# A batched x·yᵀ on one Trainium2 core: products on four 64x64 tiles of TensorE, and stores of 4 MB as two 16 KB runs per partition

## The chip, the cores and the metric

The kernel runs on one core of one Trainium2 chip. The core has five engines with their own instruction streams: TensorE (PE, with its weight loads shown as PEld), VectorE (DVE), ScalarE (ACT), GpSimd (POOL) and SyncE (SP), and 16 DMA engines that carry data between HBM and the on-chip memory of 128 partitions. Engines wait for one another through semaphores. The metric is device time in microseconds; the time before is 301.73 us, the median of 3 runs (301.65 to 301.77).

## The reference

```python
def setup_inputs():
    batch, n_heads, seq_t, seq_s, channels = 8, 12, 512, 512, 64
    return {
        "x": np.random.randn(batch, n_heads, seq_t, channels).astype(np.float32),
        "y": np.random.randn(batch, n_heads, seq_s, channels).astype(np.float32),
    }

def reference(x, y):
    return np.einsum('bhtc,bhsc->bhts', x, y).astype(np.float32)
```

There are 96 heads. For each, a 512x64 matrix times the transpose of another 512x64 matrix gives 512x512 floats. The inputs are 2 x 12.6 MB, the output 100.7 MB.

## The kernel before

**Groups, halves, turns.** Sixteen heads form a group, and there are 6 groups (`NG`). A group of x or of y is 2 MB, laid out with 64 rows of 64 channels on each of the 128 partitions: a head takes 8 partitions. Half a group (8 heads, 64 partitions) is one turn of the products; there are 12 turns (`NH`). Each turn writes 8 MB of output as two stores of 4 MB, so there are 24 stores.

**Slots.** Three slots (`slots`) of 128 partitions x 32 KB serve two purposes. At the beginning each half of a slot is the landing place of one 2 MB load: the loads are numbered n = 0 to 11, x and y of group 0, x and y of group 1, and so on, six of them at once. Later a slot holds the 16 output rows per partition (`K = 16`) of one store. Everything moved by DMA is issued by SP on one queue: loads 0 to 5 at once, loads 6 to 11 each when its slot half has been cast (L146), then the 24 stores in order (L255), each when its slot has been filled.

**Casts (`compress`).** x of a group is cast from f32 to bf16 into `xk`, whole, by ACT (by POOL for the last group). y is cast by four instructions straight into an interleaved form (`yb`): DVE takes two, POOL one, and ACT or POOL the fourth. In `yb` two rows' values lie side by side in one 32-bit word.

**Mixing of x (`mix`).** Four copies a turn bring x into `xb`, one for each 32 of the turn's 64 partitions and each 32 channels. A value takes 16 bits of a 32-bit word; the other 16 are zero, from a memset of `xb` at the start, and which half of the word is filled depends on which group of four heads the value belongs to. POOL does these copies for the first two turns, DVE from then on.

**Transposes.** DVE's transposes work on 32x32 blocks of 32-bit words: the first half of `xb` into `xT0`, `yb` into `yT`, the second half of `xb` into `xT1`. Afterwards the contraction runs over 128 partitions: 64 channels for each of two groups of four heads. In a column of x that belongs to one group of heads, the 64 partitions of the other group hold the zeros.

**Products.** PE runs one hardware loop over the 12 turns (`products`). A unit is 8 matmuls, each with 128x64 weights from `xT` and 128x512 moving values from `yT`. Two run side by side, on the two 64-column halves of TensorE (`tile_position=(0, hs * 64)`). A unit fills four banks of PSUM (`pm0` or `pm1`, in turn). PE waits on `turned`, which DVE's transposes count up, and on `taken`, which ACT counts up as it empties `pm`.

**Evictions and stores (`unit`).** ACT copies each unit from PSUM into a quarter of a slot (128x2048 floats), and after four units SP issues the store. An eviction into a slot waits for the slot's previous store to land. The orders of all engines are written out by the loops at the end of the kernel; `emit` and `need` derive the waits from what is read and written. The store's view of the output is

```python
ov = out.rearrange("b h t s -> (b h t s)").rearrange(
    "(o u t q n) -> o t q u n", u=2, t=2, q=2 * Q * E, n=K * S
)
```

so that one store takes 128 runs of 32 KB, and neighbouring partitions (`u` = 0 and 1) write 4 MB apart.

Of the kernel before, what the change touches and what calls it, by code (L numbers as in the profile page):

```python
# [10 lines left out]
def kernel(  # L11
# [22 lines left out]
    nc = tc.nc  # L34
    B, H, T, C = x.shape
    _, _, S, _ = y.shape
    P = 128
    G = 16
    Q = P // G
# [1 line left out]
    NG = B * H // G  # L41
    NH = 2 * NG
    V = G // 4
    K = 16
    E = R // K
    D = 32
    U = K // 4
    SLOTS = 3
    fp32 = mybir.dt.float32
    bf16 = mybir.dt.bfloat16  # L50
# [4 lines left out]
    xv = x.rearrange("b h t c -> (b h t c)").rearrange("(g p n) -> g p n", p=P, n=R * C)  # L55
    yv = y.rearrange("b h t c -> (b h t c)").rearrange("(g p n) -> g p n", p=P, n=R * C)
    ov = out.rearrange("b h t s -> (b h t s)").rearrange(
        "(o u t q n) -> o t q u n", u=2, t=2, q=2 * Q * E, n=K * S
    )

    sb = ctx.enter_context(tc.tile_pool(name="sb", bufs=1))
    ps = ctx.enter_context(tc.tile_pool(name="ps", bufs=1, space=bass.MemoryType.PSUM))
    slots = [sb.tile([P, K * S], fp32, name=f"slot{i}") for i in range(SLOTS)]
    xks = [sb.tile([P, R, C], bf16, name=f"xk{i}") for i in range(NG - 1)]
    ybs = [[sb.tile([P, R // 2 * D], u32, name=f"yb{h}{i}") for i in range(NG - 1 + h)] for h in range(2)]
    xb = sb.tile([P, R * D], u32, name="xb")
    xTs = [sb.tile([P, K // 2 * D * E], u32, name=f"xT{i}") for i in range(2)]
    yT = sb.tile([P, D * R // 2], u32, name="yT")
    pms = [ps.tile([P, 4, S], fp32, name=f"pm{i}") for i in range(2)]
    engines = {"act": nc.scalar, "dve": nc.vector, "pool": nc.gpsimd, "pe": nc.tensor, "sp": nc.sync}  # L70
    sems, ticks, known, snaps, writer, readers = {}, {}, {e: {} for e in engines}, {}, {}, {}
    own = {e: {} for e in engines}
# [1 line left out]
    def sem(p):  # L74
        if p not in sems:
            sems[p] = tc.alloc_semaphore(p)
        return sems[p]
# [40 lines left out]

    asked = []

    def caster(n, half, ch):
        if n % 2 == 0:
            return "pool" if n == 10 else "act"
        return ("dve", "pool", "dve", "pool" if n > 8 else "act")[2 * half + ch]

    def copy(name, dst, src, reads, writes, tells=None, virtual=False):
        emit(
            name,
# [7 lines left out]
        )  # L136

    def space(n):
        i, j = divmod(n % (2 * SLOTS), 2)
        return slots[i][:, j * (K * S // 2):(j + 1) * (K * S // 2)], [("slot", i, 2 * j), ("slot", i, 2 * j + 1)]  # L140

    def load(n):
        to, where = space(n)
        emit(
            "sp",
            lambda: nc.sync.dma_start(to, (yv if n % 2 else xv)[n // 2]),  # L146
            writes=where,
            dma=f"in{n % (2 * SLOTS)}",
        )

    def compress(n):

        g = n // 2
        held, where = space(n)
        if n % 2 == 0:
            xk = g % (NG - 1)
            dst = xks[xk].rearrange("p r c -> p (r c)")
            copy(caster(n, 0, 0), dst, held, where, [("xk", xk)])
            return
        ys = held.rearrange("p (r c) -> p r c", c=C)  # L160
        for half in range(2):
            b = g % (NG - 1 + half)
            yv2 = ybs[half][b].bitcast(bf16).rearrange("p (j c w) -> p j w c", j=R // 2, w=2)
            for ch in range(2):
                copy(
                    caster(n, half, ch),
                    yv2[ch * 64:(ch + 1) * 64],
                    ys[half * 64:(half + 1) * 64, :, ch * D:(ch + 1) * D].rearrange(
                        "p (j w) c -> p j w c", w=2
                    ),  # L170
                    where,
                    [("yb", half, b, ch)],
                )

    def mix(i, name, part):

        g, half = divmod(i, 2)
        ch, u = divmod(part, 2)
        lo = half * 64 + u * D
        xk = g % (NG - 1)  # L180
        copy(
            name,
            xb[part * D:(part + 1) * D].bitcast(bf16).rearrange("p (r c u) -> p r c u", c=D, u=2)[:, :, :, u],
            xks[xk][lo:lo + D, :, ch * D:(ch + 1) * D],
            [("xk", xk)],
            [("xb", part)],
        )

    def transposes(i):
        g, half = divmod(i, 2)  # L190
        b = g % (NG - 1 + half)
        xe = xb.rearrange("p (e k c) -> p e k c", e=E, c=D)

        def of_x(kh):
            emit(
                "dve",
                lambda: nc.vector.transpose(  # L197
                    xTs[kh].rearrange("p (k r e) -> p e k r", r=D, e=E),
                    xe[:, :, kh * (K // 2):(kh + 1) * (K // 2), :],
                ),  # L200
                [("xb", part) for part in range(4)],
                [("xT", kh)],
                tells="turned",
            )

        of_x(0)
        emit(
            "dve",
            lambda: nc.vector.transpose(  # L209
                yT.rearrange("p (r j) -> p j r", r=D),  # L210
                ybs[half][b].rearrange("p (j c) -> p j c", c=D),
            ),
            [("yb", half, b, ch) for ch in range(2)],
            ["yT"],
            tells="turned",
        )
        of_x(1)

    def products():

        pe = mybir.EngineType.PE
        xcs = [t.bitcast(bf16).rearrange("p (k h m) -> p k h m", k=K // 2, h=V) for t in xTs]
        yc = yT.bitcast(bf16)
        nc.tensor.sem_inc(sem("taken"), 2)
        with nc.Fori(0, NH, engines=OrderedEngineSet([pe])) as turn:
            for t in range(2):
                for v in range(U):
                    done = t * U + v
                    if done in (0, U // 2):
                        nc.tensor.wait_ge(sem("turned"), turn * 3 + (2 + (done > 0)))  # L230
                    nc.tensor.wait_ge(sem("taken"), turn * (2 * U) + (done + 1))
                    for j in range(4):
                        kh, k = divmod(4 * v + j, K // 2)
                        for hs in range(2):
                            h = 2 * t + hs
                            last = nc.tensor.matmul(  # L236
                                pms[v % 2][hs * 64:(hs + 1) * 64, j, :], xcs[kh][:, k, h, :], yc[:, h * S:(h + 1) * S],
                                start=True, stop=True, tile_position=(0, hs * 64),
                            )
                    last.then_inc(sem("pe"), 1)  # L240

    def unit(o, v):

        i = o // 2
        pm = v % 2
        emit("pe", None, [("xT", v // 2), "yT"], [("pm", pm)], virtual=True)
        want = {"turned": 3 * i + (2 if o % 2 == 0 and v < 2 else 3), "taken": o * U + v + 1}
        assert all(want.get(p, 0) >= w for p, w in asked[-1].items()), (o, v, asked[-1])
        s = o % SLOTS
        rows = slots[s].rearrange("p (r s) -> p r s", s=S)[:, 4 * v:4 * v + 4, :]  # L250
        copy("act", rows, pms[pm], [("pm", pm)], [("slot", s, v)], "taken")
        if v == U - 1:
            emit(
                "sp",
                lambda: nc.sync.dma_start(ov[i, o % 2], slots[s]),  # L255
                reads=[("slot", s, w) for w in range(U)],
                dma=f"out{s}",
            )

    with tc.tile_critical():  # L260
        sem("taken")
        ticks["taken"] = 2
        for n in range(2 * SLOTS):
            load(n)
        emit("pool", lambda: nc.gpsimd.memset(xb, 0.0), writes=[("xb", part) for part in range(4)])  # L265
        for n in range(2 * NG):
            compress(n)
            if n < 2 * SLOTS:
                load(n + 2 * SLOTS)
            if n < 8:  # L270
                mix(n // 4, "pool", n % 4)
            if n == 3:
                transposes(0)
            if 6 < n < 11:
                for v in (0, 1) if n % 2 else (2, 3):
                    unit((n - 7) // 2, v)
            if n == 10:
                transposes(1)
        for part in range(4):
            mix(2, "dve", part)  # L280
        for i in range(1, NH):
            for o in (2 * i, 2 * i + 1):
                for v in range(U):
                    unit(o, v)
            if i + 1 < NH:
                transposes(i + 1)
            if i + 2 < NH:
                for part in range(4):
                    mix(i + 2, "dve", part)
        products()  # L290
        for name, o in (("pe", 2 * NH - 3), ("sp", 2 * NH - 2), ("act", 2 * NH - 1)):
            need(name, [(f"out{o % SLOTS}", ticks[f"out{o % SLOTS}"])])
# [30 lines left out]
```

## Time and profile before

| what | value |
|---|---|
| median of 3 runs | 301.73 us |
| the profiled execution, its own time | 301.98 us |
| its span | 300.2 us |
| mean granted TensorE clock | 0.748 |
| PE busy | 141.6 us (47%), 768 matmuls |
| DVE busy | 156.3 us (52%), 88 instructions |
| ACT busy | 203.6 us (68%), 106 instructions |
| POOL busy | 55.8 us (19%), 22 instructions |

The costliest groups of instructions, with the number of instructions, their busy time, the mean ns of one, the idle time of the engine just before them and what ended most of it:

```profile
L129 ACT ACTIVATE slot<-pm 128x2048 f32<-128x2048 f32 x96 | 174.4, 1879 | 54.1 <-DMA out_dram<-slot 42.7
L236 PE MATMUL pm<-yT,xT 128*64 128x512 bf16 x768 | 141.6, 520 | 133.7 <-ACT slot L129 77.4
...
L197 DVE STREAM_TRANSPOSE xT<-xb 128x1024 uint32<-128x1024 uint32 x24 | 48.2, 2009 | 36.0 <-PE pm L236 33.6
...
L209 DVE STREAM_TRANSPOSE yT<-yb 128x1024 uint32<-128x1024 uint32 x12 | 23.3, 1939 | 42.4 <-PE pm L236 42.4
```

A busy share is an average over a filling part (about the first 60 us, when the loads come in and POOL is at work) and a steady part (only stores). Idle time of an engine costs nothing as long as another resource sets the pace. A DMA's time "to landing" runs from its issue to its last byte and includes the time in which it stands behind earlier transfers.

### The profile page before, as it was taken

To read this page: it belongs to the slowest core of one execution; us is meant where nothing else is said; L and a number is where in the kernel's file an instruction comes from. 1 tells how busy PE (TensorE), PEld (TensorE's weight loads), DVE (VectorE), ACT (ScalarE), POOL (GpSimd) and SP (SyncE) were. 2 spreads that over 40 slices of the span, in tenths; PEclk is the share of its full clock that TensorE was granted. 3 is DMA by queue.
4 is the path that set the end of the run, shared out by engine and by line. 5 is a ranking of instruction groups with operands and counts; after the bars stand their busy time and mean duration, and the time that the engine had idled before them with its cause. 6 is when DMAs were issued, how large, how long until landed. Compare 5 with 4: busy or idle time off the path is not lost.

```text
span 300.2 us, 2037 instructions
## 1 busy us (share of the span) xinstructions
PE 141.6 (47%) x768; PEld 47.1 (16%) x768; DVE 156.3 (52%) x88; ACT 203.6 (68%) x106; POOL 55.8 (19%) x22
## 2 busy tenths in 40 slices
PE   0000314644866664847746467457483775644000
PEld 0000101211222211212212122112121221211000
DVE  0157874889894953826539447275393562500000
ACT  1665579875979868766876678667866696669000
POOL 2399299997000000000000000000000000000000
PEclk9999985597679786675866975877758577597555
DMA  7999999999999999999999999999999999999991
GB/s 271 428 434 432 426 428 428 430 426 450 450 424 419 419 454 450 424 419 420 450 442 428 424 419 445 445 428 428 419 450 441 428 424 419 450 441 428 424 424 83
DMA packets 5186, 125.85 MB, mean 419 GB/s; under 512 B 576, under 2 KB 576, under 8 KB 576
## 3 DMA queue, kind: packets, MB, share of 16 engines
q1 hardware_dynamic: 5184, 125.83, 97.7%
q14 instruction: 2, 0.02, 0.0%
HBM read 25.17 MB, written 100.66 MB: 419 GB/s over the span
## 4 chain that ended last, share of the span: by engine, by line
DMA 46%; ACT 19%; POOL 18%; PE 5%; DVE 3%; issue 1%; ACTq 0%; POOLq 0%; SPq 0%
DMA out_dram<-slot 44%; ACT slot L129 18%; POOL xb L131 8%; POOL yb L131 8%; PE pm L236 5%; DMA slot<-in_x_dram 3%; DVE xT L197 1%; DVE yT L209 1%; ACT xk L129 1%; POOL xk L131 1%; ACTq L92 0%; POOLq L92 0%; SPq L318 0%; SPq L260 0%
## 5 line engine op out<-in xcount | busy, mean ns | idle before, releaser
L129 ACT ACTIVATE slot<-pm 128x2048 f32<-128x2048 f32 x96 | 174.4, 1879 | 54.1 <-DMA out_dram<-slot 42.7
L236 PE MATMUL pm<-yT,xT 128*64 128x512 bf16 x768 | 141.6, 520 | 133.7 <-ACT slot L129 77.4
L236 PEld LDWEIGHTS pm<-yT,xT 128*64 128x64 bf16 x768 | 47.1, 138 | 227.6 <-ACT slot L129 145.2
L197 DVE STREAM_TRANSPOSE xT<-xb 128x1024 uint32<-128x1024 uint32 x24 | 48.2, 2009 | 36.0 <-PE pm L236 33.6
L131 DVE COPY xb<-xk 32x2048 bf16<-32x2048 bf16 x40 | 55.5, 1387 | 1.3
L209 DVE STREAM_TRANSPOSE yT<-yb 128x1024 uint32<-128x1024 uint32 x12 | 23.3, 1939 | 42.4 <-PE pm L236 42.4
L131 DVE CAST yb<-slot 64x2048 bf16<-64x2048 f32 x12 | 31.7, 2645 | 23.8 <-DMA slot<-in_y_dram 23.6
L131 POOL COPY xb<-xk 32x2048 bf16<-32x2048 bf16 x8 | 25.3, 3162 | 15.7 <-ACT xk L129 9.7
L129 ACT ACTIVATE xk<-slot 128x4096 bf16<-128x4096 f32 x5 | 18.1, 3617 | 13.8 <-DMA slot<-in_x_dram 13.8
L131 POOL CAST yb<-slot 64x2048 bf16<-64x2048 f32 x8 | 24.9, 3118 | 0.9
L129 ACT ACTIVATE yb<-slot 64x2048 bf16<-64x2048 f32 x4 | 9.8, 2460 | 5.1 <-DMA slot<-in_y_dram 5.1
L131 POOL CAST xk<-slot 128x4096 bf16<-128x4096 f32 x1 | 3.6, 3595 | 0.1
L265 POOL MEMSET xb<- 128x2048 uint32 x1 | 1.8, 1805 | 0.5 <-SPq L260 0.5
L129 ACT ACT_TABLE_LOAD x1 | 1.3, 1283 | 0.9 <-SPq L260 0.9
L307 POOL MEMSET const-float32-0.0<- 128x1 f32 x1 | 0.1, 98 | 0.2 <-issue 0.2
L307 POOL MEMSET const-bfloat16-1.0<- 128x1 bf16 x1 | 0.1, 100 | 0.0
L307 POOL MEMSET const-uint8-127<- 128x1 uint8 x1 | 0.1, 100 | 0.0
L307 POOL MEMSET const-float32-1.0<- 128x1 f32 x1 | 0.1, 98 | 0.0
## 6 DMA issues: line engine op xcount, KB each, us to landing
out_dram<-slot SPq DMA_DIRECT2D x24, 4096.0 KB, 22.0
slot<-in_x_dram SPq DMA_DIRECT2D x6, 2048.0 KB, 25.4
slot<-in_y_dram SPq DMA_DIRECT2D x6, 2048.0 KB, 22.2
```

The lines of the kernel that those rows point to most:

```text
L129: lambda: nc.scalar.activation(dst, src, COPY)
L131: else engines[name].tensor_copy(dst, src),
L197: lambda: nc.vector.transpose(xTs[kh].rearrange("p (k r e) -> p e k r", r=D, e=E), xe[:, :, kh * (K // 2):(kh + 1) * (K // 2), :],),
L209: lambda: nc.vector.transpose(yT.rearrange("p (r j) -> p j r", r=D), ybs[half][b].rearrange("p (j c) -> p j c", c=D),),
L236: last = nc.tensor.matmul(pms[v % 2][hs * 64:(hs + 1) * 64, j, :], xcs[kh][:, k, h, :], yc[:, h * S:(h + 1) * S], start=True, stop=True, t ...
L265: emit("pool", lambda: nc.gpsimd.memset(xb, 0.0), writes=[("xb", part) for part in range(4)])
L307: nc = _bacc.Bacc("TRN2", target_bir_lowering=False, num_devices=1)
```

## The change

The zeros go. x and y are both cast whole into bf16 (`xks`, and new `yks`), ACT taking x of the first four groups and POOL all y and the last two x. `mix` now interleaves both: eight copies of 32x2048 a turn, all on DVE, two rows' values side by side in a word for x as for y. The two groups of four heads lie on the two 64-partition halves, so a product contracts over 64 partitions with 64x64 weights, and TensorE is used as four 64x64 tiles (`tile_position=(t * 64, hs * 64)`). `xb` and `xT` are half as large, and so are the two x transposes. Four neighbouring matmuls (`t` and `hs`) go to four tiles and two PSUM banks. The memset is gone.

A slot is now 2 x 8 rows (`K = 8`), one half for each group of heads, and a unit writes two rows into each half. A store is 4 MB as before, but each partition's 32 KB go out as two runs of 16 KB, 4 MB apart. The turn's units are ordered by pairs of heads `o`. The six late loads are issued in the same order, each after one cast of the slot half. In the filling part, the first evictions into a slot wait for the casts of both its halves. PE counts up a semaphore (`mark`) that nothing waits for, once per unit.

```diff
-    K = 16
+    K = 8
...
-    U = K // 4
+    U = K // 2
...
-        "(o u t q n) -> o t q u n", u=2, t=2, q=2 * Q * E, n=K * S
+        "(i t o p n) -> i o p t n", t=2, o=2, p=P, n=K * S
...
-    slots = [sb.tile([P, K * S], fp32, name=f"slot{i}") for i in range(SLOTS)]
+    slots = [sb.tile([P, 2, K, S], fp32, name=f"slot{i}") for i in range(SLOTS)]
     xks = [sb.tile([P, R, C], bf16, name=f"xk{i}") for i in range(NG - 1)]
-    ybs = [[sb.tile([P, R // 2 * D], u32, name=f"yb{h}{i}") for i in range(NG - 1 + h)] for h in range(2)]
-    xb = sb.tile([P, R * D], u32, name="xb")
-    xTs = [sb.tile([P, K // 2 * D * E], u32, name=f"xT{i}") for i in range(2)]
-    yT = sb.tile([P, D * R // 2], u32, name="yT")
-    pms = [ps.tile([P, 4, S], fp32, name=f"pm{i}") for i in range(2)]
+    yks = [sb.tile([P, R, C], bf16, name=f"yk{i}") for i in range(NG - 1)]
+    xb = sb.tile([P, R // 2 * D], u32, name="xb")
+    yb = sb.tile([P, R // 2 * D], u32, name="yb")
+    xTs = [sb.tile([P, K // 4 * D * E], u32, name=f"xT{i}") for i in range(2)]
+    yT = sb.tile([P, R // 2 * D], u32, name="yT")
+    pms = [ps.tile([P, 2, 2, S], fp32, name=f"pm{i}") for i in range(2)]
...
+        g, b = n // 2, n // 2 % (NG - 1)
+        name = "pool" if n % 2 or n > 7 else "act"
+        to = (yks if n % 2 else xks)[b].rearrange("p r c -> p (r c)")
+        at = ("half", n % (2 * SLOTS))
+        copy(name, to, held, [at], [("yk" if n % 2 else "xk", b)])
+        if n >= 2 * NG - 2 * SLOTS:
+            for w in where:
+                readers.setdefault(w, []).extend(readers[at][-1:])
+
+    def mix(i):
+
+        g, half = divmod(i, 2)
+        b = g % (NG - 1)
+        for kind, held, to in (("x", xks[b], xb), ("y", yks[b], yb)):
+            pairs = to.bitcast(bf16).rearrange("p (j c w) -> p j w c", j=R // 2, w=2)
+            for part in range(4):
+                u, ch = divmod(part, 2)
+                lo = half * 64 + u * D
                 copy(
...
+                    "dve",
+                    pairs[part * D:(part + 1) * D],
+                    held[lo:lo + D, :, ch * D:(ch + 1) * D].rearrange("p (j w) c -> p j w c", w=2),
+                    [(kind + "k", b)],
+                    [(kind + "b", part)],
                 )
...
+                    nc.tensor.sem_inc(sem("mark"), 1)
+                    kh, k = divmod(v, U // 2)
+                    for w in range(2):
+                        for t in range(2):
+                            rows = slice(t * 64, (t + 1) * 64)
+                            for hs in range(2):
+                                h = 2 * o + hs
+                                last = nc.tensor.matmul(
+                                    pms[v % 2][hs * 64:(hs + 1) * 64, t, w, :],
+                                    xcs[kh][rows, k, w, h, :], yc[rows, h * S:(h + 1) * S],
+                                    start=True, stop=True, tile_position=(t * 64, hs * 64),
+                                )
...
-        copy("act", rows, pms[pm], [("pm", pm)], [("slot", s, v)], "taken")
+        copy("act", slots[s][:, :, 2 * v:2 * v + 2, :], pms[pm], [("pm", pm)], [("slot", s, v)], "taken")
...
-                lambda: nc.sync.dma_start(ov[i, o % 2], slots[s]),
+                lambda: nc.sync.dma_start(ov[i, o % 2], slots[s].rearrange("p t k s -> p t (k s)")),
...
-        emit("pool", lambda: nc.gpsimd.memset(xb, 0.0), writes=[("xb", part) for part in range(4)])
...
-            if n < 8:
-                mix(n // 4, "pool", n % 4)
-            if n == 3:
+            if n == 1:
+                mix(0)
                 transposes(0)
-            if 6 < n < 11:
-                for v in (0, 1) if n % 2 else (2, 3):
+                mix(1)
+            if n > 6 and n % 2:
+                for v in range(U):
                     unit((n - 7) // 2, v)
-            if n == 10:
+            if n == 9:
                 transposes(1)
-        for part in range(4):
-            mix(2, "dve", part)
+                mix(2)
...
             if i + 2 < NH:
-                for part in range(4):
-                    mix(i + 2, "dve", part)
+                mix(i + 2)
```

More of the change, by code (lines that the diff above doesn't have):

```diff
@@ L119 @@
     asked = []
[L121 to L124, printed above, removed]
     def copy(name, dst, src, reads, writes, tells=None, virtual=False):
@@ L138, in space @@
     def space(n):
-        i, j = divmod(n % (2 * SLOTS), 2)
-        return slots[i][:, j * (K * S // 2):(j + 1) * (K * S // 2)], [("slot", i, 2 * j), ("slot", i, 2 * j + 1)]
+        i, t = divmod(n % (2 * SLOTS), 2)
+        return slots[i][:, t].rearrange("p k s -> p (k s)"), [("slot", i, v) for v in range(U)]
     def load(n):
-        to, where = space(n)
+        to, _ = space(n)
         emit(
@@ L146, in load @@
             lambda: nc.sync.dma_start(to, (yv if n % 2 else xv)[n // 2]),
-            writes=where,
+            writes=[("half", n % (2 * SLOTS))],
             dma=f"in{n % (2 * SLOTS)}",
@@ L151, in compress @@
     def compress(n):
-        g = n // 2
         held, where = space(n)
[L155 to L164, printed above, removed]
-                copy(
[L166 to L172, printed above, removed]
-                )
@@ L175, in mix @@
[L175 to L187, printed above, removed]
+        g, b = n // 2, n // 2 % (NG - 1)
+        name = "pool" if n % 2 or n > 7 else "act"
@@ L189, in transposes @@
     def transposes(i):
-        g, half = divmod(i, 2)
-        b = g % (NG - 1 + half)
         xe = xb.rearrange("p (e k c) -> p e k c", e=E, c=D)
+        kk = K // 4
         def of_x(kh):
@@ L198, in of_x @@
                     xTs[kh].rearrange("p (k r e) -> p e k r", r=D, e=E),
-                    xe[:, :, kh * (K // 2):(kh + 1) * (K // 2), :],
+                    xe[:, :, kh * kk:(kh + 1) * kk, :],
                 ),
@@ L210, in transposes @@
                 yT.rearrange("p (r j) -> p j r", r=D),
-                ybs[half][b].rearrange("p (j c) -> p j c", c=D),
+                yb.rearrange("p (j c) -> p j c", c=D),
             ),
-            [("yb", half, b, ch) for ch in range(2)],
+            [("yb", part) for part in range(4)],
             ["yT"],
@@ L221, in products @@
         pe = mybir.EngineType.PE
-        xcs = [t.bitcast(bf16).rearrange("p (k h m) -> p k h m", k=K // 2, h=V) for t in xTs]
+        xcs = [t.bitcast(bf16).rearrange("p (k h m w) -> p k w h m", k=K // 4, h=V, w=2) for t in xTs]
         yc = yT.bitcast(bf16)
@@ L225, in products @@
         with nc.Fori(0, NH, engines=OrderedEngineSet([pe])) as turn:
-            for t in range(2):
+            for o in range(2):
                 for v in range(U):
-                    done = t * U + v
+                    done = o * U + v
                     if done in (0, U // 2):
@@ L231, in products @@
                     nc.tensor.wait_ge(sem("taken"), turn * (2 * U) + (done + 1))
[L232 to L239, printed above, removed]
+                    nc.tensor.sem_inc(sem("mark"), 1)
[10 more added lines that the diff above has]
+                                )
                     last.then_inc(sem("pe"), 1)
@@ L245, in unit @@
         pm = v % 2
-        emit("pe", None, [("xT", v // 2), "yT"], [("pm", pm)], virtual=True)
-        want = {"turned": 3 * i + (2 if o % 2 == 0 and v < 2 else 3), "taken": o * U + v + 1}
+        emit("pe", None, [("xT", v // (U // 2)), "yT"], [("pm", pm)], virtual=True)
+        want = {"turned": 3 * i + (2 if o % 2 == 0 and v < U // 2 else 3), "taken": o * U + v + 1}
         assert all(want.get(p, 0) >= w for p, w in asked[-1].items()), (o, v, asked[-1])
         s = o % SLOTS
-        rows = slots[s].rearrange("p (r s) -> p r s", s=S)[:, 4 * v:4 * v + 4, :]
-        copy("act", rows, pms[pm], [("pm", pm)], [("slot", s, v)], "taken")
+        copy("act", slots[s][:, :, 2 * v:2 * v + 2, :], pms[pm], [("pm", pm)], [("slot", s, v)], "taken")
         if v == U - 1:
@@ L264 @@
             load(n)
[L265 removed]
         for n in range(2 * NG):
             compress(n)
[L268 removed]
+            if n < 2 * NG - 2 * SLOTS:
                 load(n + 2 * SLOTS)
[L270 to L272 removed]
+            if n == 1:
+                mix(0)
                 transposes(0)
[L274 to L275 removed]
+                mix(1)
+            if n > 6 and n % 2:
+                for v in range(U):
                     unit((n - 7) // 2, v)
[L277 removed]
+            if n == 9:
                 transposes(1)
[L279 to L280 removed]
+                mix(2)
         for i in range(1, NH):
@@ L283 @@
                 for v in range(U):
-                    unit(o, v)
+                    if o > 2:
+                        unit(o, v)
             if i + 1 < NH:
```

## The prediction, made before the changed kernel ran

> **What bounds the kernel now.** I read the page's transfer rows first, because the span is 300.2 us and the whole traffic is fixed by the problem: 25.17 MB in, 100.66 MB out.
>
> ```profile
> DMA  7999999999999999999999999999999999999991
> ...
> q1 hardware_dynamic: 5184, 125.83, 97.7%
> ...
> HBM read 25.17 MB, written 100.66 MB: 419 GB/s over the span
> ```
>
> The 16 DMA engines are occupied in every slice but the first and the last, for 97.7% of the span. All 36 transfers go through one queue, so the time is: first packet, then 125.83 MB at the engines' pace, then the end of the slowest engine. The next view cuts the span into stretches (columns: PE, PEld, DVE, ACT, POOL busy, granted clock, DMA share, GB/s): all loads, then stores alone, then the end.
>
> ```profile
> 10.00:60.00 50.00, 11.88 (x54) 3.92 (x56) 32.70 (x14) 36.75 (x15) 40.84 (x13) 0.83 1.01 429
> 85.00:280.00 195.00, 115.40 (x638) 38.64 (x634) 100.94 (x64) 145.29 (x80) 0.00 (x0) 0.74 1.00 432
> 292.50:295.00 2.50, 0.00 (x0) 0.00 (x0) 0.00 (x0) 0.00 (x0) 0.00 (x0) 0.50 0.55 236
> 295.00:297.50 2.50, 0.00 (x0) 0.00 (x0) 0.00 (x0) 0.00 (x0) 0.00 (x0) 0.50 0.06 26
> ```
>
> Two things are to be seen. Loads, whose packets are 16 KB, run at 429 GB/s; stores, whose packets are 32 KB, at 432. And the end is ragged: in the last row the share is 0.06, which is one engine of sixteen, still writing when fifteen have finished. The packet records behind this view give the sizes: on fifteen engines successive 32 KB store packets start 1,209 to 1,210 ns apart all the way; on one engine they start 1,234 ns apart on average, but only while the cores compute (from 280 us on it is back to about 1,210). Over 192 store packets that is 192 x 24 ns = 4.6 us, part of which it had gained before: it ends at 298.6 us, the others at 294.0 to 294.7.
>
> Is the queue ever short of work? The chain of waits and the waits of the queue's own engine answer it:
>
> ```profile
> 218.25 21.95 DMA out_dram<-slot
> ...
> 240.29 1.89 ACT slot L129
> 242.17 0.04 issue
> 242.22 1.94 PE pm L236 x8
> 244.15 0.02 issue
> 244.18 3.65 ACT slot L129 x2
> ...
> 247.85 22.04 DMA out_dram<-slot
> ```
>
> ```profile
> SPq L255 <- ACT slot L129: 220.6, 24, 12.9
> ```
>
> The chain shows a slot's round: a store takes 22 us from issue to landing, then evictions refill the slot in about 7.6 us. SP waits 220.6 us for ACT, which looks like a bound and is none: a 4 MB store needs 4.19 MB / 432 GB/s = 9.7 us by itself, so at its issue 22.0 - 9.7 = 12.3 us of earlier stores stand before it. An eviction that comes 12 us late costs nothing.
>
> **The change, part by part.**
>
> *Stores as two 16 KB runs per partition.* Each 4 MB store becomes 256 packets instead of 128, so each engine writes 24 x 16 = 384 store packets in place of 192. No 16 KB write exists in the trace; the nearest row is the 16 KB load. Its starts are 607.7 ns apart where the loads run cleanest (10 to 20 us) and 611.5 ns between 30 and 60 us. Two of them against one 32 KB packet: 2 x 607.7 - 1,209.4 = 6.0 ns, or 2 x 611.5 - 1,210 = 13 ns. Per engine that is 192 x 6.0 = 1.15 us, or 192 x 13 = 2.5 us. The coarse rates agree: 100.66 MB at 429 instead of 432 GB/s is 234.6 against 233.0, 1.6 us. Lower bound: 0, if what the loads lose is the reading of HBM and not the packet. A gain I exclude, since no row shows a smaller packet moving more. I take 1.15 us, the cleanest stretch, where the fewest other things ran. All of it lies on the path, because the queue is never empty.
>
> The Trainium skill, page "DMA: Bandwidth & Descriptors", section "Latency and other measured facts", speaks against this part: it reports rows 4 MiB apart falling to 103 GB/s. Here the two runs of a partition are 4 MB apart. The row: the stores of now already send neighbouring partitions (`u`) 4 MB apart and run at 432 GB/s. By the rule the stores would take 100.66 MB / 103 GB/s = 977 us; I go by the row, since packets that alternate between the two regions are already what is measured.
>
> *The lagging engine.* What slows it the trace does not say; it goes with computing. After the change the same bytes are written while the same 768 matmuls and 96 evictions run, with DVE's count up from 88 instructions to 132 and POOL's down. I take the lag as it is, 4 us. Bounds: 0 (it vanishes, -4 us) and, if the loss is per packet and not per time, double (+4.6 us). For the range I take a third of each side as reachable.
>
> *DVE does all mixing.* Before, DVE interleaves x alone (4 copies a turn) and casts part of y. Now 8 copies of 32x2048 a turn, 96 in all, plus three transposes, of which the two x ones have half the elements. The price of a copy into this interleaved pattern is in two rows:
>
> ```profile
> L131 DVE COPY xb<-xk x40: 1296/1320/3420, 71.1 to 244.0; 32x2048 bf16<-32x2048 bf16 x40
> ...
> L131 DVE CAST yb<-slot x12: 1296/2912/3454, 13.6 to 67.6; 64x2048 bf16<-64x2048 f32 x12
> ```
>
> The cast has exactly the new nesting (32, 2, 32) on the output side; it runs at 1,296 ns when POOL is quiet (the one at 36.61 us) and up to 3,454 beside POOL. So 1.32 us with POOL idle, 3.45 at most beside it. In steady state, POOL has finished by about 70 us: 8 x 1.32 + 1.94 (y transpose) + 2 x 1.0 (half of 2,009 ns) = 14.5 us a turn. A turn's two stores need 19.4 us. Hidden under the stores; cover left 4.9 us a turn, and 12.3 us of queued stores behind that.
>
> *TensorE on four 64x64 tiles.* A unit is still 8 matmuls of 512 columns, now four at a time instead of two: 0.97 us or so instead of 1.94 at the low clock (the chain's x8 row). If the row halves don't overlap it stays at 1.94. Either way it sits beside ACT's 1.88 us per unit, and PE was idle half the span. Nothing on the path. After the last unit of a turn, 1.94 (y transpose) + 0.2 + 1 us pass before ACT has new work, against 1.88 of its own still running, so ACT's turn is about 8 x 1.83 + 1.3 = 16 us, under 19.4. The semaphore increment `mark` adds 8 PE instructions a turn there.
>
> *The fill.* POOL now casts every y (3.6 us by its x row; 5.0 if slowed like its y casts, 3.3 against 2.45), ACT the first four x. The evictions of store 0 now wait for both halves of their slot: y of group 3 lands at 43 (DVE's wait for it ends at 42.95), cast by 46.6 to 48, four evictions of 1.88 us, so store 0 is issued at 54 to 55.5; before it was at 57.0. The queue's loads end at 61.6 to 62. On DVE: first y cast by 17.2 to 18.6, then 8 copies beside POOL for about a third of the time (8 x 1.32 to 8 x 2.2 = 11 to 18 us) and 4 us of transposes; the first products start at 32 to 40, ahead of 47. Store 1 waits for y of group 4 (lands 52.7, cast by 58): 65.5 against 71.3 needed. Store 2: y of group 5 by 68, evictions by 75.5 against 81. SP passes loads 6 to 11 in the same order, each behind one cast: 12.3, 18.6, 22.1, 28.4, 31.9, 38.2 at the latest, none much later than now (last one 43.7). POOL loses the 1.8 us memset and the x copies. No packet comes later for any of it.
>
> **Sum.** Span 300.2 + 1.15 = 301.4; the profiled execution's own time was 301.98 against a median of 301.73, 0.25 above, so I add the change to the median: 301.73 + 1.15 = 302.9 us.
>
> **Rivals.**
> 1. *Not slower: the lagging engine catches up.* Place: the end, 294.7 to 298.6. Price up to -3.9 us. For it: the lag exists only beside computing, and PE's busy time falls from 141.6 us to perhaps half. Against: ACT's work and the number of instructions stay. From a cut of 1.15 us of the 3.9 (30%) it decides the sign; with two thirds gone, 301.73 + 1.15 - 2.6 = 300.3 us.
> 2. *The smaller packets cost nothing,* the loads' pace being HBM reading: 301.7 us. For it: the fit of 6 ns is small; against: the clean stretch shows it on all sixteen engines.
> 3. *DVE becomes the bound:* copies at 2.4 us instead of 1.32 even with POOL idle. Then a turn is 8 x 2.4 + 4 = 23.2 us; ten turns from 62 us, then 4 + 16 + 12 for the last: 330 us. Against: the 1,296 ns row with that nesting. The four products not overlapping at all (8 x 0.43 = 3.4 us a unit, 27.5 a turn) would end above that, near 380.
> 4. *The lag is per packet* and doubles: 302.9 + 4 = 307.
>
> **Chances.** Forecast 0.58; rival 1 0.17, rival 2 0.13, rival 4 0.06, rival 3 0.06. The time is the forecast's, 302.9. Its own range, from the packet's 0 to 2.5 us and a tenth of the lag, is 301.8 to 304.4; with a third of the lag on each side the range that holds 8 in 10 is 300.9 to 305.2. About 0.2% (0.6 us) is what a measurement here can tell from no change: slower than 302.3 has 0.70 (forecast, 3, 4), within 0.2% 0.13 (rival 2), faster 0.17.
>
> **What would show it.** Store packets of 16 KB with the stores' stretch at 429 to 431 GB/s: the packet step. Store packets starting 605 ns apart or less: wrong (rival 2). A last stretch with share 0.06 of about 4 us: the lag as it is; 0.06 absent or twice as long: rivals 1 or 4. DVE copies near 1.32 us and DVE idle waiting for PE: hidden; DVE never idle and a DMA digit below 9 in the middle: rival 3. A store 0 issued after 61.6 us would make the fill wrong.

## The result, and the profile after

The changed kernel takes 302.88 us (median of 6 runs, 302.63 to 303.42) against 301.75 us for the one before on the same chips (301.65 to 302.15): ratio 1.0037, 95% interval 1.0024 to 1.0050. It is slower by 1.1 us, about as forecast. The profiled execution took 302.99 us with a span of 301.2 us.

First the DMA's share and the transfer row of the page, then the stretches of the stores (columns: length, the five engines' busy time and counts, granted clock, DMA share, GB/s), after and, behind it, before. A packet is counted whole in the row in which it starts.

```profile
DMA  7999999999999999999999999999999999999993
...
q1 hardware_dynamic: 8256, 125.83, 98.3%
```

```profile
85.00:180.00 95.00, 40.27 (x316) 9.51 (x312) 68.61 (x54) 69.30 (x39) 0.00 (x0) 1.00 1.01 430
200.00:280.00 80.00, 32.04 (x248) 7.14 (x240) 42.68 (x33) 57.48 (x32) 0.00 (x0) 1.00 1.01 426
...
292.50:295.00 2.50, 0.00 (x0) 0.00 (x0) 0.00 (x0) 0.00 (x0) 0.00 (x0) 1.00 1.03 439
295.00:297.50 2.50, 0.00 (x0) 0.00 (x0) 0.00 (x0) 0.00 (x0) 0.00 (x0) 1.00 0.36 151
297.50:300.00 2.50, 0.00 (x0) 0.00 (x0) 0.00 (x0) 0.00 (x0) 0.00 (x0) 1.00 0.05 20
```

```profile
85.00:180.00 95.00, 57.68 (x330) 19.79 (x328) 56.24 (x36) 72.40 (x40) 0.00 (x0) 0.75 1.00 431
200.00:280.00 80.00, 45.67 (x246) 14.95 (x242) 33.67 (x22) 58.21 (x32) 0.00 (x0) 0.71 1.00 433
...
297.50:300.00 2.50, 0.00 (x0) 0.00 (x0) 0.00 (x0) 0.00 (x0) 0.00 (x0) 0.50 0.00 0
```

The queue carries 8,256 packets instead of 5,184, the 3,072 more that two runs per partition make. It is still never empty. The stores run at 430 GB/s up to 180 us and at 426 after 200 us; before, the same two stretches had 431 and 433. The end is as ragged as it was, nearly one engine's 0.06 in the last row, only later. The packet records give each packet's start, duration and size but not its engine; strung together by their times they make sixteen rows of packets. Fifteen engines end at 296.2 us (the median of them) instead of 294.2, and the late one at 299.6 instead of 298.6. So the path moved by 1.0 us, while the other fifteen engines lost 2.0.

DVE's work and its waits:

```profile
L127 DVE COPY xb<-xk x48: 1277/1296/4700, 12.2 to 243.1; 32x2048 bf16<-32x2048 bf16 x48
...
L127 DVE COPY yb<-yk x48: 1280/1301/4655, 20.9 to 248.5; 32x2048 bf16<-32x2048 bf16 x48
```

```profile
DVE yT L195 <- PE pm L225: 52.1, 11, 5.9
```

A copy takes 1.30 us in the steady part, and DVE waits 4.7 us a turn for PE (52.1 us over 11 turns): the copies are hidden. The slowest copies, beside POOL, took 4.7 us, longer than the 3.45 that I had as their bound; the reason is told below.

### The profile page after: what moved, and what is told of

The parts are those of the page before. It is cut to its first block, busy times and chain, and to the rows that moved or that the text cites. A ratio compares the mean times of both kernels' runs of the same rounds, so it can differ in the third digit from the quotient of the medians.

```text
span 301.2 us, 2167 instructions
## 1 busy us (share of the span) xinstructions
PE 99.9 (33%) x768; PEld 23.4 (8%) x768; DVE 189.8 (63%) x132; ACT 188.1 (62%) x101; POOL 31.3 (10%) x12
## 3 DMA queue, kind: packets, MB, share of 16 engines
q1 hardware_dynamic: 8256, 125.83, 98.3%
## 4 chain that ended last, share of the span: by engine, by line
DMA 69%; ACT 19%; POOL 2%; SPq 1%; issue 0%; ACTq 0%
DMA out_dram<-slot 51%; ACT slot L125 19%; DMA slot<-in_y_dram 18%; POOL yk L127 2%; SPq L142 1%; ACTq L93 0%; SPq L305 0%; SPq L249 0%
## 5 line engine op out<-in xcount | busy, mean ns | idle before, releaser
L125 ACT ACTIVATE slot<-pm 128x2048 f32<-128x2048 f32 x96 | 172.4, 1884 | 64.2 <-DMA out_dram<-slot 54.0
L225 PE MATMUL pm<-yT,xT 64*64 64x512 bf16 x768 | 99.9, 627 | 175.8 <-ACT slot L125 120.2
L127 DVE COPY xb<-xk 32x2048 bf16<-32x2048 bf16 x48 | 69.8, 1453 | 13.7 <-ACT xk L125 12.2
L127 DVE COPY yb<-yk 32x2048 bf16<-32x2048 bf16 x48 | 72.5, 1511 | 1.5
L195 DVE STREAM_TRANSPOSE yT<-yb 128x1024 uint32<-128x1024 uint32 x12 | 23.3, 1944 | 52.1 <-PE pm L225 52.1
L225 PEld LDWEIGHTS pm<-yT,xT 64*64 64x64 bf16 x768 | 23.4, 140 | 251.5 <-issue 251.5
L125 ACT ACTIVATE xk<-slot 128x4096 bf16<-128x4096 f32 x4 | 14.5, 3617 | 24.9 <-DMA slot<-in_x_dram 24.9
L183 DVE STREAM_TRANSPOSE xT<-xb 128x512 uint32<-128x512 uint32 x24 | 26.2, 1090 | 1.8 <-PE pm L225 1.5
L127 POOL CAST yk<-slot 128x4096 bf16<-128x4096 f32 x6 | 22.8, 3792 | 33.0 <-DMA slot<-in_y_dram 32.8
L127 POOL CAST xk<-slot 128x4096 bf16<-128x4096 f32 x2 | 8.3, 4175 | 1.5 <-DMA slot<-in_x_dram 1.5
```

The costliest lines, as they stand in the source:

```text
L125: lambda: nc.scalar.activation(dst, src, COPY)
L127: else engines[name].tensor_copy(dst, src),
L183: lambda: nc.vector.transpose(xTs[kh].rearrange("p (k r e) -> p e k r", r=D, e=E), xe[:, :, kh * kk:(kh + 1) * kk, :],),
L195: lambda: nc.vector.transpose(yT.rearrange("p (r j) -> p j r", r=D), yb.rearrange("p (j c) -> p j c", c=D),),
L225: last = nc.tensor.matmul(pms[v % 2][hs * 64:(hs + 1) * 64, t, w, :], xcs[kh][rows, k, w, h, :], yc[rows, h * S:(h + 1) * S], start=True, ...
```

## The experiments

Each run's time stands beside that of the kernel before on the same chip, 301.77 to 301.83 us. Where the end of the queue is given, it is from the packet records of the profiled execution: the median end of the fifteen engines, and the end of the late one. Where an experiment changes only into how many runs a partition's 32 KB are split, rows of the output land in other places than the reference has them.

**One run per partition again.** The changed kernel's computing with the old packets.

```diff
-        "(i t o p n) -> i o p t n", t=2, o=2, p=P, n=K * S
+        "(i o p n) -> i o p n", o=2, p=P, n=2 * K * S
...
-                lambda: nc.sync.dma_start(ov[i, o % 2], slots[s].rearrange("p t k s -> p t (k s)")),
+                lambda: nc.sync.dma_start(ov[i, o % 2], slots[s].rearrange("p t k s -> p (t k s)")),
```

> The changed kernel, but each partition's 32 KB of a store go to one contiguous run of the output (rows land in other places than the reference has them; bytes, stores and everything before them are the same). Theory (each extra store packet costs 5 to 6 ns of every DMA engine, the slowest one included, and nothing else of the change reaches the path): 1.1 us back, 301.6 to 302.0, store packets 1,210 ns apart, the last engine at about 298.6 us. Rival (the casts, copies and 64x64 products cost the time, or the lagging engine changed with them): stays at 302.7 to 303.2.

Measured: 302.19 us (301.99 to 302.68), ratio to before 1.0013 (1.0004 to 1.0023). Neither theory alone: 0.7 us of the 1.1 comes back, 0.4 us stays. The fifteen engines are back at 294.1 us, but the late one ends at 299.0, later than the 298.6 of before.

```profile
295.00:297.50 2.50, 0.00 (x0) 0.00 (x0) 0.00 (x0) 0.00 (x0) 0.00 (x0) 1.00 0.06 26
297.50:300.00 2.50, 0.00 (x0) 0.00 (x0) 0.00 (x0) 0.00 (x0) 0.00 (x0) 1.00 0.03 13
```

This is the end of that run: one engine alone in both rows, where in the kernel before no packet starts in the second. Fifteen engines end as before and the late one 0.4 us later, so the new computing lengthens the lag.

**Two runs in the kernel before.** The mirror image: old computing, new packets.

```diff
-        "(o u t q n) -> o t q u n", u=2, t=2, q=2 * Q * E, n=K * S
+        "(i t o p n) -> i o p t n", t=2, o=2, p=P, n=K * S // 2
...
-                lambda: nc.sync.dma_start(ov[i, o % 2], slots[s]),
+                lambda: nc.sync.dma_start(ov[i, o % 2], slots[s].rearrange("p (t n) -> p t n", t=2)),
```

> The kernel before, with its stores written as two 16 KB runs 4 MB apart (rows land in other places than the reference has them; all else as before). Theory: 302.6 to 303.2, all of the change's loss without any of its computing. Rival: 301.7, as before. In either case it shows whether the packets' wider spacing after about 180 us (607 to 614 ns), which the changed kernel's records have, belongs to the 16 KB packets or to the new computing.

Measured: 302.22 us (302.10 to 302.63), ratio 1.0013 (1.0004 to 1.0023): 0.4 us. The fifteen engines end at 296.1 us, the late one at 299.2. The wider spacing (426 GB/s from 200 to 280 us, as in the changed kernel) is there too, so it belongs to the packets and not to the new computing.

**Four runs of 8 KB.**

```diff
-        "(i t o p n) -> i o p t n", t=2, o=2, p=P, n=K * S
+        "(i t o p n) -> i o p t n", t=4, o=2, p=P, n=K * S // 2
...
-                lambda: nc.sync.dma_start(ov[i, o % 2], slots[s].rearrange("p t k s -> p t (k s)")),
+                lambda: nc.sync.dma_start(ov[i, o % 2], slots[s].rearrange("p t k s -> p (t k s)").rearrange("p (t n) -> p t n", t=4)),
```

> The changed kernel with its stores as four 8 KB runs per partition, 2 MB apart (rows land in other places than the reference has them). Theory with a fixed price per packet: 384 more packets per engine at 5 to 6 ns, 1.9 to 2.3 us more than the changed kernel, 304.8 to 305.2. Rival (the loss is in having two runs, not in the number of packets): 302.9.

Measured: 303.98 us (303.92 to 304.10), ratio 1.0070 (1.0053 to 1.0086), 1.1 us more than the changed kernel; less than the 1.9 expected. The price per packet is there on the fifteen engines, 2 x 305.9 - 607.4 = 4.4 ns per extra packet where the spacing is even, and more after that: they end at 300.4 us. The late engine ends at 300.8 us, 0.4 us behind them. So from two to four runs the fifteen engines lost 4.2 us and the late one 1.2: a price per packet shows in the time only in part as long as there is a lag. Why the late engine loses less than the others, no run shows.

**Half the products.**

```diff
-                    for w in range(2):
+                    for w in range(1):
```

(plus two memsets of PSUM at the start; half of the output rows are never computed).

> The changed kernel with half the matmuls (one of two row pairs is never computed; PSUM is cleared once by two memsets at the start, so half the output rows are stale or zero). It asks what the engine that ends last depends on. If its loss goes with PE's instructions (1,536 of 2,167): the lag of 3.4 us falls to about 2 and the time to 301.3 to 301.7. If it goes with ACT's evictions, DVE's copies or the stores themselves: no change, 302.6 to 303.2.

Measured: 301.03 us (300.84 to 301.67), ratio 0.9976 (0.9964 to 0.9987), 1.85 us less than the changed kernel and faster than the one before. The fifteen engines end where they did (296.2 us); the late one at 297.8 instead of 299.6.

```profile
295.00:297.50 2.50, 0.00 (x0) 0.00 (x0) 0.00 (x0) 0.00 (x0) 0.00 (x0) 1.00 0.39 164
297.50:300.00 2.50, 0.00 (x0) 0.00 (x0) 0.00 (x0) 0.00 (x0) 0.00 (x0) 1.00 0.00 0
```

The last row is empty now. The lag goes with PE's work, in data or in instructions; 1.85 us / 766 instructions would be 2.4 ns each.

**Instructions without data.**

```diff
-                    nc.tensor.sem_inc(sem("mark"), 1)
+                    for _ in range(9):
+                        nc.tensor.sem_inc(sem("mark"), 1)
```

> The changed kernel with PE counting `mark` nine times per unit instead of once: 768 more PE instructions that move no data and that nothing waits for. Halving the matmuls took 766 instructions away and 1.85 us. If the last engine's loss goes with the number of instructions executed (2.4 ns each): 1.85 us more, 304.5 to 305.0, lag of the last engine 4.5 to 5.5 us. Rival (it goes with the data that the matmuls read and write): 302.7 to 303.2.

Measured: 305.31 us (305.11 to 305.55), ratio 1.0119 (1.0102 to 1.0136), 2.4 us more than the changed kernel for 768 instructions that move nothing: 3.2 ns each. The fifteen engines have not moved (296.2 us), the late one ends at 301.7.

```profile
297.50:300.00 2.50, 0.00 (x0) 0.00 (x0) 0.00 (x0) 0.00 (x0) 0.00 (x0) 1.00 0.06 26
300.00:302.50 2.50, 0.00 (x0) 0.00 (x0) 0.00 (x0) 0.00 (x0) 0.00 (x0) 1.00 0.03 13
```

Compared with the rows above, one engine is busy for a whole slice longer. So the data is not needed: the number of PE's instructions executed while stores go out slows one of the sixteen engines. Instructions of other engines were not varied by themselves. Why that engine, the runs don't tell.

**Leaving one engine out of the last store.** If the late engine could be spared at the end, its lag would be free. The last store is cut into 120 and 8 partitions (the edit of the kernel before; the changed kernel has the same cut):

```diff
+            for lo, hi in ((0, 120), (120, 128)) if o == 2 * NH - 1 else ((0, 128),):
...
+                    lambda: nc.sync.dma_start(ov[i, o % 2][lo // 2:hi // 2], slots[s][lo:hi]),
```

> The kernel before, with its last store cut in two: 120 partitions, then the last 8. If a transfer of 120 partitions is spread over fifteen engines and the late engine is the one left out, that engine gets 8 packets (9.7 us) less and the eight partitions fall to four others (2.4 us more each): the end moves from 298.6 to about 297, the time to 299.8 to 300.4. If the late engine is one of the fifteen, it is no faster: 301.7, or up to 304.2 where it also gets some of the eight partitions.

> The changed kernel with the same cut of its last store; its eight partitions fall to eight engines (1.2 us more each). Late engine left out: the end moves from 299.6 to about 297.5, the time to 300.5 to 301.1. Late engine not left out: 302.9 to 304.2.

Measured: 309.55 us (309.44 to 309.73) in the kernel before, ratio 1.0256 (1.0239 to 1.0273), and 311.92 us in the changed one, ratio 1.0344 (1.0325 to 1.0363). Both are far outside the expected ranges.

```profile
270.00:280.00 10.00, 3.69 (x16) 1.11 (x16) 0.00 (x0) 7.05 (x4) 0.00 (x0) 0.50 1.00 433
...
290.00:300.00 10.00, 0.00 (x0) 0.00 (x0) 0.00 (x0) 0.00 (x0) 0.00 (x0) 0.50 0.81 210
```

The rate of the cut store is 210 GB/s, half of the full one, while the engines count as busy for 81%: many 32 KB packets take 2,300 to 2,550 ns instead of 1,210. The last store, cut in this way, goes at half speed; whether that comes from its 120 partitions or from the cut, the runs don't separate. The packet records still answer the question asked. In the kernel before, sixteen engines are at work until 284.5 us and fifteen from 285 to 293.5: one was left out, and it ended at 284.8 us. The late engine without its last eight packets would have ended at about 298.6 - 8 x 1.21 = 288.9. In the changed kernel the one left out ended at 286.6, where the late one would have ended at about 289.8. So a punctual engine was left out, both times, and the idea was not put to the test.

**The packet's number or the time.** The first twelve stores with one run, the last twelve with two:

```diff
+    ow = out.rearrange("b h t s -> (b h t s)").rearrange("(i o p n) -> i o p n", o=2, p=P, n=2 * K * S)
...
-                lambda: nc.sync.dma_start(ov[i, o % 2], slots[s].rearrange("p t k s -> p t (k s)")),
+                lambda: nc.sync.dma_start(ow[i, o % 2], slots[s].rearrange("p t k s -> p (t k s)"))
+                if i < NH // 2
+                else nc.sync.dma_start(ov[i, o % 2], slots[s].rearrange("p t k s -> p t (k s)")),
```

> The changed kernel with its first 12 stores written as one 32 KB run per partition (rows land in other places than the reference has them) and the last 12 as two of 16 KB. In the runs so far the 16 KB and 8 KB packets are evenly spaced until about the 300th packet of an engine (186 us with 16 KB, 128 us with 8 KB), then wider. If it goes with the packet's number, the wider spacing begins at about 245 us here (96 + 96 + 16 a store); if with the time or the place in the output, at once with the 13th store, at about 180 us. Time: 302.2 to 302.9 (between one run's 302.19 and two runs' 302.88).

Measured: 302.53 us (302.42 to 302.92), ratio 1.0026 (1.0016 to 1.0037), in the expected range.

```profile
200.00:240.00 40.00, 16.88 (x132) 3.87 (x128) 29.04 (x23) 28.74 (x16) 0.00 (x0) 1.00 1.00 430
260.00:280.00 20.00, 6.40 (x48) 1.30 (x48) 0.00 (x0) 14.37 (x8) 0.00 (x0) 1.00 1.01 428
```

The two-run stores keep 430 GB/s until 240 us, where the changed kernel has 426 from 200 us on. In the packet records the spacing is 607.0 to 607.4 ns up to an engine's 300th packet (244 us), 608 around the 320th, and 610 to 614 from the 336th on. It goes with how many packets an engine has moved, not with the time; what in that number matters is open.

**More copies on DVE.**

```diff
-        for kind, held, to in (("x", xks[b], xb), ("y", yks[b], yb)):
+        for kind, held, to in (("x", xks[b], xb), ("x", xks[b], xb), ("y", yks[b], yb)):
```

> The changed kernel with the four x copies of every turn done twice. DVE then has 12 x 1.30 + 2 x 1.09 + 1.94 = 19.7 us of work a turn against 19.4 to 19.6 us of stores. Theory (DVE hidden behind queued stores of some 12 us): no more than the 48 instructions' 0.15 us, 302.8 to 303.3. Rival (DVE was near the bound already): 306 or more.

Measured: 305.16 us (304.97 to 305.31), ratio 1.0112 (1.0097 to 1.0128): 2.3 us more than the changed kernel, between the two. The page's chain and a stretch of the filling part:

```profile
DVE 63%; ACT 17%; issue 9%; PE 3%; DMA 3%; SPq 0%
```

```profile
80.00:82.50 2.50, 1.36 (x12) 0.22 (x8) 2.44 (x3) 2.50 (x3) 0.00 (x0) 1.00 0.34 144
```

The chain has gone from DMA to DVE, and the queue ran dry for 2.5 us at 81 us, in wait of the third store. So DVE's room was thin in the filling part, where its copies take up to 4.7 us beside POOL, and not in the steady part, where the four copies nearly fitted. Once the queue has run dry, turns of 19.75 us of DVE's work set the pace.

Doubling all eight (`(("x", xks[b], xb), ("y", yks[b], yb)) * 2`):

> The changed kernel with all eight copies of every turn done twice: DVE has 16 x 1.30 + 2 x 1.09 + 1.94 = 24.9 us a turn, 5.4 us more than the stores. The cover of 12 us is used up after two or three turns, then DVE sets the pace: ten turns of 24.9 us from about 66 us on, then 16 us of evictions and 12 us of the last store, 340 to 348 us. If less than 330, a turn has more room than the sum says.

Measured: 365.02 us (364.97 to 365.07), ratio 1.2094 (1.2072 to 1.2116). DVE is the bound, as expected; the time is 17 us over my range because I let the chain of turns start at 66 us, though with double copies the second turn's mixing, from 47.5 us on and in part beside POOL, takes 31 us, so that its transposes are done only at 82.3 us.

**Fewer instructions, whole output.** In the kernel before, 8 rows per partition instead of 16 make a product with full 128x128 weights: half the matmuls and weight loads, at the price of 16 KB runs and of 48 stores of 2 MB instead of 24 of 4 MB.

```diff
-    K = 16
+    K = 8
...
-                        kh, k = divmod(4 * v + j, K // 2)
-                        for hs in range(2):
-                            h = 2 * t + hs
...
+                        hs, kh = divmod(v, 2)
+                        h = 2 * t + hs
+                        last = nc.tensor.matmul(
+                            pms[v % 2][:, j, :], xcs[kh][:, j, h, :], yc[:, h * S:(h + 1) * S],
+                            start=True, stop=True,
+                        )
...
+                lambda: nc.sync.dma_start(ov[i, 2 * (o % 2) + hs], slots[s][:, hs * K * S:(hs + 1) * K * S]),
```

> The kernel before with half its PE instructions and the whole output: 8 instead of 16 rows per partition, so that one product has 128x64 zero-padded weights for each of two row sets, 128x128 in one weight load, 384 matmuls instead of 768. Each 4 MB store becomes two of 2 MB with 16 KB runs. Theory (the last engine's loss goes with the number of instructions, 2.4 ns each by the halved products and 3.2 ns by the nine marks; 16 KB packets cost 0.4 us net): 301.8 + 0.4 - 1.8 to 2.4 = 299.8 to 300.4, lag of the last engine 1 to 2 us. Rival (full 128x128 products, or smaller stores, bring a loss of their own): 301.5 or more.

Measured: 301.30 us (301.10 to 301.65, 11 runs) against 301.83, ratio 0.9984 (0.9975 to 0.9993). It beats both kernels, but by 0.5 us instead of the 1.4 to 2.0 expected. The lag fell as expected (the fifteen engines end at 295.9 us, the late one at 297.6), but I had charged the packets with 0.4 us, which is their price behind a lag of 4 us. With a small lag more of the fifteen engines' 2 us seems to come out; the next run bears on it. PE is as busy as in the kernel before (143.3 against 141.6 us), so the lag does not go with PE's busy time.

**The same with one run per partition.**

```diff
-        "(o u h q n) -> o h q u n", u=2, h=4, q=Q * E, n=K * S
+        "(o h p n) -> o h p n", h=2, p=P, n=2 * K * S
```

(and the two stores of 2 MB made one).

> The kernel of half the PE instructions (full rows), with its stores of 4 MB in one contiguous 32 KB run per partition again (rows land in other places than the reference has them). If the two costs are separate, the fifteen engines end as in the kernel before (about 294.2 us) and the last one 1.2 to 1.8 us later, so the end moves from 298.6 to about 295.7 and the time to 298.7 to 299.5. If the last engine's lag and the packets' size go together (a smaller lag only because the others are slower), 300.5 or more.

Measured: 300.02 us (299.91 to 300.14), ratio 0.9943 (0.9926 to 0.9959): 0.5 us above the expected range, and below the 300.5 of the other reading. The fifteen engines end at 294.0 us, the late one at 296.5, 2.5 us behind instead of the 1.2 to 1.8. Against the kernel before, 768 instructions fewer bring 1.8 us, 2.3 ns each. Against the run above, the smaller packets, together with the 24 additional stores, cost 1.3 us here, where the packets alone cost 0.4 us in the kernel before.

## Why the prediction was right

*The bound* was the queue and its late engine, as read. The queue is never empty in the changed kernel, and every run that moved the time without emptying it moved the end of those sixteen engines. The forecast of 302.9 us met the measured 302.88; that it is so close is luck, since two of its terms were off and made up for each other.

*The packet's price* was read rightly on the fifteen engines where the spacing is even, somewhat high: 2 x 607.4 - 1,210 = 4.8 ns per extra packet, 0.9 us in place of 1.15. But I put it on the path whole, and the path belongs to the late engine. There it shows with 0.4 us (old computing) to 0.7 us (new computing), in place of 1.15. The fifteen lost 2.0 us, half of it by the wider spacing after the 300th packet, which no row of before could show, because an engine had 288 data packets in all.

*The lag taken as it was* is the step that failed in size: the term was 0 and is about 0.4 us. I listed DVE's 44 additional instructions and the 96 `mark`s and gave them no price, since they sit on idle engines. The price of an instruction is not its engine's time but, by the runs that varied PE's, 2.3 to 3.2 ns on one DMA engine. If every instruction costs as much, 2,167 instead of 2,037 make 0.3 to 0.4 us, and the run with one run per partition measured 0.4 for all of the new computing. So the sum of 1.1 us is made of 0.4 for the computing, which I had at 0, and 0.7 for the packets, which I had at 1.15.

*DVE.* The rows of before gave the right price, 1.30 against my 1.32 us, and a turn with room: 4.7 us of waiting against my 4.9. The bound of 3.45 us beside POOL was too low (4.7 us), and it sits where the room is thinnest, as the doubled copies showed. I had taken it from the longest row of before, as if POOL slowed DVE's copies by a factor. The rows show another thing:

```profile
23.30 3.70 POOL L127 CAST yk<-slot 128x4096 bf16<-128x4096 f32 x1 [6.19 <-DMA slot<-in_y_dram]
```

```profile
23.57 5.90 DVE L127 COPY yb<-yk 32x2048 bf16<-32x2048 bf16 x2
```

The first of these two copies ends at 28.14 us, 1.14 us after POOL's cast, and the second, with POOL idle, takes 1.30. All six slow copies of the changed kernel end 1.14 to 1.23 us after a cast of POOL, and all twelve slow casts and copies of DVE beside POOL in the kernel before 1.14 to 1.19 us after an instruction of POOL. So a copy that begins during a POOL instruction waits for its end, and the bound follows the length of that instruction: 3.6 + 1.14 = 4.7 us with the new casts. The cast at 36.61 us that I took for one with POOL quiet was not: POOL's copy began 0.3 us behind it, and it was POOL that took longer (3.31 instead of 2.44 us).

*The fill.* Store 0 was issued at 53.9 us (54 to 55.5 predicted), the first products began at 32.6 (32 to 40), and the third store's evictions ended at 73.4 (75.5). Nothing came late to the queue.

*TensorE.* 0.97 us per unit was forecast, 1.07 was measured, and by another way, told below, so that the nearness is luck. Nothing of it is on the path.

*The rivals.* The catching-up engine (rival 1) was half of the truth with the wrong sign: the lag does depend on computing, on the number of PE's instructions and not on PE's busy time, which fell from 141.6 to 99.9 us while the lag, at equal packets, grew. Packets that cost nothing (rival 2) and a lag per packet (rival 4) are out by the runs with one, two and four runs. DVE as the bound (rival 3) is out by its waits for PE. The fall to 103 GB/s that the prediction weighed for the runs 4 MB apart is not seen: 430 GB/s.

*Two sums* of the prediction don't come out as written: a packet's 0 to 2.5 us and a tenth of the lag make a range of 301.3 to 304.6 us, not 301.8 to 304.4, and rival 3's first case adds up to 326 us, not 330. Neither changes what was forecast.

## What to carry to other kernels

When the DMA engines are full from end to end, look at which of the sixteen ends last, since a price that all pay counts only as far as the slowest one pays it. On such a kernel, work on idle engines is not quite free, at least as measured here, with every execution recorded: each PE instruction cost 2 to 3 ns at the end of the queue, so larger instructions and fewer of them won more (1.8 us) than half as many packets did in either kernel (0.4 and 0.7 us). And before adding work to an engine with room in the steady part, check its room in the filling part, beside the engine that it has to wait for.

## What the runs showed that was not expected

- One DMA engine of sixteen slows with the number of PE's instructions executed, with data or without: halving the matmuls took 1.85 us off, 768 empty semaphore counts added 2.4 us. It is seen only while stores go out; in the loads' part all sixteen keep pace. In the packet records of the ten kernels whose queue never ran dry and whose last store is whole, the time by which store packets outlast the usual one, summed over a stretch of stores with even spacing and divided by the instructions recorded in that stretch, is 2 to 3.4 ns, with 5 to 12 recorded instructions per microsecond. The cause stays open. Every execution here was recorded, so writing the records is a rival that no run separates from the instructions themselves, and an execution without recording may have no such lag.
- Store packets of 16 KB are 607.4 ns apart up to about the 300th packet of an engine and 610 to 615 ns after it; of 8 KB, 306 and then 309 to 314. It came at about 128, 190 and 255 us in three kernels, each time at 300 to 330 packets. The cause is open.
- The store cut into 120 and 8 partitions ran at 210 GB/s, half the rate of one over 128.
- A DVE copy that begins during a POOL cast stands still until it ends (1.14 us of the copy's 1.30 are left then), rather than going on more slowly.
- Four 64x64 products at once brought PE no speed where its clock was full. The units of both kernels, from the timelines, at granted clock 1.0:

```profile
125.41 1.05 PE L236 MATMUL pm<-yT,xT 128*64 128x512 bf16 x8 [0.19 <-ACT slot L129]
```

```profile
124.16 1.07 PE L225 MATMUL pm<-yT,xT 64*64 64x512 bf16 x8 [2.88 <-ACT slot L125]
```

A unit takes 1.05 us with two products at a time and 1.07 with four. What changed is the clock: the mean granted clock was 0.748 before and 1.0 after. At granted clock 0.50 a unit of the kernel before took 1.94 us (the one at 242.22 us in the prediction's chain). Why the clock rose, no run was made to show.
